# Sliding attention with the values stationary: two heads side by side, outputs transposed, probabilities normalised first

## The chip, the cores and the metric

One core of one Trainium2 chip runs the whole program in one launch. The metric is the device time of that launch in microseconds (us). PE is the matrix engine, PEld its weight loads, DVE the vector engine, ACT the scalar engine, POOL the general engine; SP only issues DMAs here.

## What is computed

The input is 256 tokens of width 1024 in fp32. Two layers of a first block (dilated and differential attention) are followed by two layers of a second block, and each of those runs two branches from one wide projection: a gated delta rule, and sliding attention with a sink, which is all that the change touches. Its 16 query heads of width 64 share 2 key/value heads, 8 to each; a query sees the 128 tokens up to and with itself.

```python
scores = einsum(qb, kw) * 64 ** -0.5            # 2 blocks of 128 queries
scores = where(mask, scores, -inf)              # 0 <= query - key < 128
m = maximum(max(scores), sink)                  # sink: one number per head
p = exp(scores - m)
probs = p / (sum(p) + exp(sink - m))
o = einsum(probs, vw)                           # 64 columns per head
y_b = o.reshape(256, 16 * 64) @ w_up_sw
...
mix = (sigmoid(gate_a) * y_a + sigmoid(gate_b) * y_b) @ w_o
x = x + rmsnorm(mix, post_mix_g)
ff = square(relu(rmsnorm(x) @ w_ff1)) @ w_ff2
x = x + rmsnorm(ff, post_mlp_g)
```

## The kernel before

All weights stream from HBM in pieces of 256 x 512. Each fp32 product of a projection is made of three matmuls in the faster fp32r format: a piece is split into `hi` (ACT, L284) and `lo` (DVE, L285), the activations are held as such a pair too (`lhi`, `llo`), and hi·hi, lo·hi and hi·lo are added up (L312 to L314, or L353 to L355 where the weights are the stationary operand). Three pieces of raw and four of split weights may be ahead of PE.

Everything that is not a projection is laid between the projection's matmuls by a planner in plain Python. `at(k, fn)` puts a step into a heap with a due time `k` units ahead, and `tick(0.5)` after every three-matmul step (after every six in the other form) moves the clock on and emits what has come due. So the due times alone set the order in which the instructions are written, and each engine runs its own instructions strictly in that order.

Sliding attention (`swa`, `windowed`) has two groups of 8 heads in each layer, and a head has four steps, with a new head every 2.1 units:

- `s_`: four fp32r matmuls give the scores (L495, L496); DVE masks them and takes their maxima (L500, two instructions with two register reads) and works out the bias of the exponent (`nm`, L1276).
- `e_`, 1.5 units later: ACT writes the exponentials into the tile `e` (L1284, 128 queries by 256 keys for the second block of queries, by 128 for the first) and their sums into `den`; POOL adds the sink's share to `den` (L1288).
- `t_`, at 2.8: PE turns `e` in three transposes (L507), ACT copies the result to SBUF as `ptS` (L509).
- `v_`, at 3.7: three fp32 matmuls (L513 to L515) hold 128 x 128 blocks of the turned probabilities stationary and move 64 columns of `vS` past them. The output `o` has queries on partitions.

After every fourth head DVE takes the reciprocals of 8 sums (L1303) and scales `o` into the tile `y`, named `tok` in the profile (L1305, twice). After every eighth head `to_lh` turns two blocks of `y`: four transposes (L371), a copy by ACT to `lhi` (L376) and the rest by DVE to `llo` (L378). The pair `lb` is then the input of the projection by `w_up_sw`.

Besides the attention the same stretch holds the delta rule's work: the convolution (L990, L993), small inversions of triangular matrices (L1138 to L1192) and the turned queries `qk` (L446, L461, L462). PSUM gives three buffers to the short-lived results of all these (tag `wk`, with scores, transposes and inversions), four to the projections and one to `o`.

Of the kernel before, what the change touches and what calls it, by code (L numbers as in the profile page):

```python
# [12 lines left out]
F32 = mybir.dt.float32  # L13
F32R = mybir.dt.float32r
I32 = mybir.dt.int32
AF = mybir.ActivationFunctionType
ALU = mybir.AluOpType
# [60 lines left out]
def body(ctx: ExitStack, tc: tile.TileContext, I, out, upto=None):  # L78
    nc = tc.nc
    V, S, G, T = nc.vector, nc.scalar, nc.gpsimd, nc.tensor  # L80
# [22 lines left out]
    def tb_(name):  # L103
        o, n = _WHERE[name]
        return tab[:, o - n0:o - n0 + n]
# [25 lines left out]
    def wk(shape, name="wk", tag="wk", bufs=3):  # L131
        return ps.tile(shape, F32, name=name, tag=tag, bufs=bufs)
# [52 lines left out]
    rope2 = [const.tile([128, 2, 16], F32, name=n) for n in ("cc2", "ss2")]  # L185
# [45 lines left out]
    def at(k, fn):  # L231
        heapq.heappush(due, (clk[0] + k, seq[0], fn))
        seq[0] += 1
# [7 lines left out]
    def tick(n=1.0):  # L241
        feed()
        pump(clk[0] + n)
# [6 lines left out]
    def tiny(n, name="tiny", bufs=4):  # L250
        return sm.tile([128, n], F32, name=name, tag=f"{name}{n}", bufs=bufs)
# [46 lines left out]
    def piece():  # L298
        if not splits:
            feed()  # L300
        return splits.popleft()

    def release():
        count["done"] += 1

    def acc2():
        return [ps.tile([128, 512], F32, name="acc", tag="acc", bufs=4) for _ in range(2)]
# [8 lines left out]
    def proj(lh, evac, sweep=False):  # L316

        acc = acc2()
        if not sweep:
            for c in range(8):  # L320
                if c % 2 == 0:
                    hi, lo, n = piece()
                for t in range(2):
                    mm3(acc[t], n, lh, c, t, hi, lo, c % 2, c == 0, c == 7)
                    if t and c % 2:
                        release()
                    if c == 7:
                        evac(acc[t], t)
                    tick(0.5)
        else:  # L330
            pieces = []
            for t in range(2):
                for c in range(8):
                    if t == 0 and c % 2 == 0:
                        pieces.append(piece())
                    hi, lo, n = pieces[c // 2]
                    mm3(acc[t], n, lh, c, t, hi, lo, c % 2, c == 0, c == 7)
                    if t and c % 2:
                        release()
                    if c == 7:  # L340
                        evac(acc[t], t)
                    tick(0.5)
# [24 lines left out]
    def to_lh(lh, src, c0, t, scale=None):  # L367

        p = wk([128, 4, 128], "tp")
        for a in range(4):  # L370
            T.transpose(p[:, a, :], src[:, a * 128:(a + 1) * 128], ident)  # L371
        sl = slice(t * 128, (t + 1) * 128)
        if scale is None or isinstance(scale, float):
            s = 1.0 if scale is None else scale
            h = lh[0][:, c0:c0 + 4, sl]
            S.activation(h, p, AF.Copy, scale=s)  # L376
            if scale is None:
                V.tensor_tensor(out=lh[1][:, c0:c0 + 4, sl], in0=p, in1=h.bitcast(F32), op=ALU.subtract)  # L378
            else:
                for a in range(4):  # L380
                    V.scalar_tensor_tensor(lh[1][:, c0 + a, sl], p[:, a, :], s, lh[0][:, c0 + a, sl].bitcast(F32),
                                           op0=ALU.mult, op1=ALU.subtract)
        else:
            for a in range(4):
                S.activation(lh[0][:, c0 + a, sl], p[:, a, :], AF.Copy, scale=scale[:, c0 + a:c0 + a + 1])  # L385
            for a in range(4):
                w = scale[:, c0 + a:c0 + a + 1]
                V.scalar_tensor_tensor(lh[1][:, c0 + a, sl], p[:, a, :], w, lh[0][:, c0 + a, sl].bitcast(F32),  # L388
                                       op0=ALU.mult, op1=ALU.subtract)
# [61 lines left out]
    def halves(i):  # L451
        return slice(64 * i, 64 * i + 64), slice(64 - 64 * i, 128 - 64 * i)

    def into_stack(dst, r, tabs):


        def then(p, cols, t):
            for i in range(2):
                a, b = halves(i)
                h = dst[a, i:8:2, cols]  # L460
                S.activation(h, p[a], AF.Copy)  # L461
                V.tensor_tensor(out=dst[b, i:8:2, cols], in0=p[a], in1=h.bitcast(F32), op=ALU.subtract)  # L462
        return turned(r, tabs, then, 4)
# [23 lines left out]
    SPL = ((0, 256), (256, 384))  # L487
# [16 lines left out]
    def probs_T(p):  # L504
        pt = wk([128, 384], "pt")
        for j in range(3):
            T.transpose(pt[:, j * 128:(j + 1) * 128], p[:, j * 128:(j + 1) * 128], ident)  # L507
        r = sm.tile([128, 384], F32, name="ptS", tag="ptS", bufs=2)
        S.activation(r, pt, AF.Copy)  # L509
        return r  # L510

    def pv_mm(o1, o0, pt, v, cols):
        T.matmul(o1, pt[:, 0:128], v[:, 0, cols], start=True, stop=False)  # L513
        T.matmul(o1, pt[:, 128:256], v[:, 1, cols], start=False, stop=True)
        T.matmul(o0, pt[:, 256:384], v[:, 0, cols], start=True, stop=True)  # L515
# [359 lines left out]
    def layer2(l, last):  # L875
        lh = nxt["lh"]
# [6 lines left out]
        vS = act.tile([128, 2, 128], F32, name="vS", tag="vS", bufs=1)  # L883
# [380 lines left out]

        lane = [0.0]

        def windowed(q, g, y):
            st = {}

            def s_(h):  # L1270
                if h % 4 == 0:
                    st["den", h // 4] = tiny(8, "den")
                s, mx = scores(q[:, h, :], kTs[0][:, g, :], kTs[1][:, g, :], tb_("bs"))
                nm = tiny(2, "nm")
                hs = 8 * g + h
                V.tensor_scalar(nm, mx, -0.125, nsink[:, hs:hs + 1], op0=ALU.mult, op1=ALU.min)  # L1276
                st["s", h] = s, nm

            def e_(h):
                den, i, hs = st["den", h // 4], h % 4, 8 * g + h  # L1280
                s, nm = st.pop(("s", h))
                e = e_tile()
                for j, (a, b) in enumerate(SPL):
                    S.activation(e[:, a:b], s[:, a:b], AF.Exp, bias=nm[:, j:j + 1], scale=0.125,  # L1284
                                 accum_out=den[:, 2 * i + j:2 * i + j + 1])
                es = tiny(2, "es")
                S.activation(es, nm, AF.Exp, bias=sinks[:, 16 * l + hs:16 * l + hs + 1])
                G.tensor_tensor(out=den[:, 2 * i:2 * i + 2], in0=den[:, 2 * i:2 * i + 2], in1=es, op=ALU.add)  # L1288
                st["p", h] = e

            def t_(h):
                st["pt", h] = probs_T(st.pop(("p", h)))

            def v_(h):
                hh, i = h // 4, h % 4
                if i == 0:
                    st["o"] = wk([128, 4, 2, 64], "o", "o", 1)
                o = st["o"]
                pv_mm(o[:, i, 0, :], o[:, i, 1, :], st.pop(("pt", h)), vS, slice(64 * g, 64 * g + 64))
                if i < 3:  # L1300
                    return
                rd = tiny(8, "rd")
                V.reciprocal(rd, st["den", hh])  # L1303
                for j in range(2):
                    V.tensor_tensor(out=y[:, 1 - j, 256 * hh:256 * hh + 256].rearrange("p (h d) -> p h d", d=64),  # L1305
                                    in0=o[:, :, j, :],
                                    in1=rd.rearrange("p (h t) -> p t h", t=2)[:, j, :, None].to_broadcast([128, 4, 64]),
                                    op=ALU.mult)
                if hh == 1:
                    for t in range(2):  # L1310
                        at(1.6 + t, lambda t=t: to_lh(sw["lb"], y[:, t, :], 4 * g, t))

            for h in range(8):
                k = max(4, lane[0] - clk[0])
                at(k, lambda h=h: s_(h))
                at(k + 1.5, lambda h=h: e_(h))
                at(k + 2.8, lambda h=h: t_(h))
                at(k + 3.7, lambda h=h: v_(h))
                lane[0] = clk[0] + k + 2.1

        m1, fins, end = [], [], 0.0
# [5 lines left out]
        sw = {}  # L1327

        def swa(g):
            q = qk_tile([8, 256], F32R)  # L1330
            if g == 0:
                sw["lb"] = new_lh()
            y, evac = into_stack(q, None, rope2)
            proj(lh, evac)
            windowed(q, g, y)

        for hh in range(2):
            qkn = dn_qk(hh)
# [43 lines left out]
        lh, r = nxt["lh"], nxt["r"]  # L1382
# [111 lines left out]
    p = wk([128, 512])  # L1494
# [50 lines left out]
```

## Time and profile before

| | us |
|---|---|
| median of 3 runs | 1742.82 |
| the runs | 1741.65 to 1745.22 |
| the profiled execution | 1741.27 |
| its span | 1739.5 |

The span is what the profiler saw between the first and the last instruction of that one execution, 1.8 us less than its time. Start times below count from the start of the span; a duration is one instruction's or that of several merged ones (x3). Ends of matmuls are modelled and overlap the next, so what a matmul costs on PE is read from the starts of neighbours. The mean granted TensorE clock is 0.99 of full speed. The second block's sliding attention is spread over 840 to 950 us in the first of its layers, and over 1357 to 1470 us in the second.

### The profile page before, as it was taken

The numbers are of one execution on the slowest core, as the hardware profiler recorded it, in microseconds if no ns is written. First come the engines' busy times: TensorE is split into PE (matmuls) and PEld (weight loads), VectorE is DVE, ScalarE is ACT, GpSimd is POOL, SyncE is SP. The second block draws the span as 40 slices with busy tenths as digits, with TensorE's granted clock in tenths as the row PEclk, the third lists the DMA queues.
The fourth block names the chain that finished last, engine by engine and source line by source line (L and its number), as shares of the span: only waits on it lengthen the run. The fifth ranks groups of instructions, "written<-read, shape, count | busy, mean of one in ns | idle before, by whom it ended". The sixth has DMA issues, their size and how long they took to land.

```text
span 1739.5 us, 26865 instructions
## 1 busy us (share of the span) xinstructions
PE 1705.6 (98%) x9865; PEld 1484.6 (85%) x9865; DVE 1169.9 (67%) x2189; ACT 996.4 (57%) x1786; POOL 268.1 (15%) x507
## 2 busy tenths in 40 slices
PE   8999999999999999999999999999999999999998
PEld 6788888888888888898889889998998888889997
DVE  5676776666777766788585676555788584775554
ACT  6666665466666654665665455445565666464443
POOL 2112321031123200320220000000320210010000
PEclk9999999999999999999999999999999999999999
DMA  6655465466655565554332655665554333646564
GB/s 206 196 173 167 152 189 173 159 195 181 177 164 155 172 192 174 168 166 134 96 104 86 197 167 182 194 193 170 160 170 140 87 102 93 198 158 195 184 184 140
DMA packets 158932, 282.27 MB, mean 162 GB/s; under 512 B 20560, under 2 KB 28496, under 8 KB 158800
## 3 DMA queue, kind: packets, MB, share of 16 engines
q1 hardware_dynamic: 157840, 277.83, 53.0%
q0 software_dynamic: 720, 2.62, 0.4%
q8 instruction: 78, 1.28, 0.3%
q14 instruction: 54, 0.44, 0.1%
q10 hardware_dynamic: 240, 0.09, 0.0%
HBM read 270.53 MB, written 1.59 MB: 156 GB/s over the span
## 4 chain that ended last, share of the span: by engine, by line
PE 51%; DVE 5%; issue 1%; ACT 1%; POOL 0%; DMA 0%; DVEq 0%; POOLq 0%; SPq 0%; ACTq 0%
PE acc L314 6%; PE acc L312 6%; PE acc L313 6%; PE acc L353 5%; PE acc L354 5%; PE acc L355 5%; PE facc L313 3%; PE facc L312 3%; PE facc L314 3%; DVE lo L285 2%; DVE hcv L993 1%; PE inv L1177 1%; PE inv L1167 1%; PE tp L371 1%; PE pt L507 1%
## 5 line engine op out<-in xcount | busy, mean ns | idle before, releaser
L285 DVE TENSOR_TENSOR lo<-raw,hi 128x1024 fp32r<-128x1024 f32 (+1 forms) x504 | 617.3, 1231 | 343.9 <-ACT hi L284 328.1
L284 ACT ACTIVATE hi<-raw 128x1024 fp32r<-128x1024 f32 (+1 forms) x504 | 527.3, 1052 | 357.5 <-PE acc L314 149.0
L312 PE MATMUL acc<-hi,lhi 128*128 128x512 f32 (+1 forms) x1344 | 550.4, 410 | 1.2 <-ACT lhi L385 1.2
L314 PE MATMUL acc<-hi,llo 128*128 128x512 f32 (+1 forms) x1344 | 526.2, 392 | 0.4 <-DVE llo L388 0.3
L313 PE MATMUL acc<-lo,lhi 128*128 128x512 f32 (+1 forms) x1344 | 524.2, 390 | 0.6 <-DVE lo L285 0.5
L314 PEld LDWEIGHTS acc<-hi,llo 128*128 128x128 f32 x1344 | 253.5, 189 | 57.4 <-DVE llo L388 3.4
L313 PEld LDWEIGHTS acc<-lo,lhi 128*128 128x128 f32 x1344 | 255.3, 190 | 41.3 <-DVE lo L285 2.0
L312 PEld LDWEIGHTS acc<-hi,lhi 128*128 128x128 f32 x1344 | 255.0, 190 | 39.7 <-ACT lhi L385 1.4
L353 PE MATMUL acc<-lhi,hi 128*128 128x256 f32 x832 | 239.1, 287 | 0.0
L355 PE MATMUL acc<-lhi,lo 128*128 128x256 f32 x832 | 235.4, 283 | 0.0
L354 PE MATMUL acc<-llo,hi 128*128 128x256 f32 x832 | 235.4, 283 | 0.0
L353 PEld LDWEIGHTS acc<-lhi,hi 128*128 128x128 f32 x832 | 159.5, 192 | 1.2 <-issue 0.4
L354 PEld LDWEIGHTS acc<-llo,hi 128*128 128x128 f32 x832 | 159.5, 192 | 0.7
L355 PEld LDWEIGHTS acc<-lhi,lo 128*128 128x128 f32 x832 | 159.4, 192 | 0.0
L312 PE MATMUL facc<-hi,fh 128*128 128x512 f32 x256 | 99.8, 390 | 0.0
L313 PE MATMUL facc<-lo,fh 128*128 128x512 f32 x256 | 99.8, 390 | 0.0
L314 PE MATMUL facc<-hi,fl 128*128 128x512 f32 x256 | 99.6, 389 | 0.0
L509 ACT ACTIVATE ptS<-pt 128x384 f32<-128x384 f32 x80 | 39.2, 490 | 82.0 <-PE pt L507 81.8
L546 POOL TENSOR_SCALAR pf<-pss 128x1 f32<-128x1 f32 x8 | 3.7, 458 | 467.6 <-ACT pj L860 467.6
L500 DVE CUSTOM_DVE_ANT_0 s<-sc,tab 128x256 f32<-128x256 f32 x192 | 60.4, 352 | 11.2 <-PE sc L496 10.6
L993 DVE SCALAR_TENSOR_TENSOR hcv<-acc,cw,hcv 128x255 f32<-128x255 f32 (+1 forms) x144 | 58.2, 475 | 1.5 <-ACT hcv L990 1.4
L314 PEld LDWEIGHTS facc<-hi,fl 128*128 128x128 f32 x256 | 48.1, 188 | 10.1
(306 smaller groups left out, 2206.9 us busy)
## 6 DMA issues: line engine op xcount, KB each, us to landing
raw<-in_w_in_dram SPq DMA_DIRECT2D x272, 512.0 KB, 3.8
raw<-in_w_ff_dram SPq DMA_DIRECT2D x128, 512.0 KB, 4.4
raw<-in_w_proj_a_dram SPq DMA_DIRECT2D x16, 512.0 KB, 3.9
raw<-in_w_proj_b_dram SPq DMA_DIRECT2D x16, 512.0 KB, 3.7
raw<-in_w_out_dram SPq DMA_DIRECT2D x16, 512.0 KB, 3.7
raw<-in_w_up_sw_dram SPq DMA_DIRECT2D x16, 512.0 KB, 3.7
raw<-in_w_up_dn_dram SPq DMA_DIRECT2D x16, 512.0 KB, 3.7
raw<-in_w_o_dram SPq DMA_DIRECT2D x16, 512.0 KB, 3.8
```

The costliest lines, as they stand in the source:

```text
L284: S.activation(hi[:, :, :o], raw[:, :, :o], AF.Copy)
L285: V.tensor_tensor(out=lo[:, :, :o], in0=raw[:, :, :o], in1=hi[:, :, :o].bitcast(F32), op=ALU.subtract)
L312: T.matmul(a, lh[0][:, c, sl], hi[:, cc, :n], start=first, stop=False)
L313: T.matmul(a, lh[0][:, c, sl], lo[:, cc, :n], start=False, stop=False)
L314: T.matmul(a, lh[1][:, c, sl], hi[:, cc, :n], start=False, stop=last)
L353: T.matmul(a, hi[:, c % 2, sl], lh[0][:, c, :], start=(c == 0 and m % 2 == 0), stop=False)
L354: T.matmul(a, hi[:, c % 2, sl], lh[1][:, c, :], start=False, stop=False)
L355: T.matmul(a, lo[:, c % 2, sl], lh[0][:, c, :], start=False, stop=(c == 7 and m % 2 == 1))
L371: T.transpose(p[:, a, :], src[:, a * 128:(a + 1) * 128], ident)
L500: V.tensor_tensor_reduce(s[:, a:b], sc[:, a:b], bias[:, a:b], 1.0, FMIN, ALU.add, ALU.max, accum_out=mx[:, j:j + 1])
L509: S.activation(r, pt, AF.Copy)
L993: V.scalar_tensor_tensor(ha[:, m, d:], a[:, m, :256 - d], tap(3 - d, m), ha[:, m, d:], op0=ALU.mult, op1=ALU.add)
```

## The change

The order of the product is turned round. The values of one key/value head, 64 columns of `vS`, are the stationary operand, and the turned probabilities move past them, so the output has the head's 64 dimensions on partitions and queries in the free dimension. That is the layout of `lhi` and `llo` already. Two heads share the array: the first uses columns 0 to 63 and partitions 0 to 63 of `o`, the second the other half. A pair of heads has four matmuls, two that move 256 columns (L1312) and two that move 128 (L1315). After every fourth head ACT writes two pieces of `lhi` (L1322) and DVE two of `llo` (L1323) straight from `o`. The tile `y`, the reciprocals and scalings by query (L1303, L1305) and the transposes of `to_lh` for this branch go.

Since queries are no longer on partitions there, the probabilities are divided by their sums before they are turned: the new step `n_`, 2.4 units after `s_`, takes the reciprocal of two sums (L1293) and scales `e` in place (L1295, once for 256 columns and once for 128), all on DVE. `t_` moves from 2.8 to 3.6 units, `v_` from 3.7 to 4.6, where it does its work at every second head only. Line numbers past L1330 are 12 higher than before. All in all PE has 8264 instructions in its order instead of 8336, DVE 1596 instead of 1512.

```diff
--- before.py
+++ after.py
@@ -1264,7 +1264,7 @@
 
         lane = [0.0]
 
-        def windowed(q, g, y):
+        def windowed(q, g):
             st = {}
 
             def s_(h):
@@ -1288,34 +1288,47 @@
                 G.tensor_tensor(out=den[:, 2 * i:2 * i + 2], in0=den[:, 2 * i:2 * i + 2], in1=es, op=ALU.add)
                 st["p", h] = e
 
+            def n_(h):
+                rd, i, e = tiny(2, "rd"), h % 4, st["p", h]
+                V.reciprocal(rd, st["den", h // 4][:, 2 * i:2 * i + 2])
+                for j, (a, b) in enumerate(SPL):
+                    V.tensor_scalar(e[:, a:b], e[:, a:b], rd[:, j:j + 1], None, op0=ALU.mult)
+
             def t_(h):
-                st["pt", h] = probs_T(st.pop(("p", h)))
+                st["pt", h] = probs_T(st.pop(("p", h))).rearrange("p (a c) -> p a c", a=3)
 
             def v_(h):
-                hh, i = h // 4, h % 4
-                if i == 0:
-                    st["o"] = wk([128, 4, 2, 64], "o", "o", 1)
-                o = st["o"]
-                pv_mm(o[:, i, 0, :], o[:, i, 1, :], st.pop(("pt", h)), vS, slice(64 * g, 64 * g + 64))
-                if i < 3:
+
+                if h % 2 == 0:
                     return
-                rd = tiny(8, "rd")
-                V.reciprocal(rd, st["den", hh])
-                for j in range(2):
-                    V.tensor_tensor(out=y[:, 1 - j, 256 * hh:256 * hh + 256].rearrange("p (h d) -> p h d", d=64),
-                                    in0=o[:, :, j, :],
-                                    in1=rd.rearrange("p (h t) -> p t h", t=2)[:, j, :, None].to_broadcast([128, 4, 64]),
-                                    op=ALU.mult)
-                if hh == 1:
-                    for t in range(2):
-                        at(1.6 + t, lambda t=t: to_lh(sw["lb"], y[:, t, :], 4 * g, t))
+                if h % 4 == 1:
+                    st["o"] = wk([128, 2, 256], "o", "o", 1)
+                o, pr = st["o"], h // 2 % 2
+                pts = [st.pop(("pt", h - 1)), st.pop(("pt", h))]
+                for blk in range(2):
+                    for i, pt in enumerate(pts):
+                        w = o[64 * i:64 * i + 64, pr, :]
+                        if blk == 0:
+                            T.matmul(w.rearrange("p (t c) -> p t c", t=2), vS[:, 0, 64 * g:64 * g + 64], pt[:, 0:3:2, :],
+                                     start=True, stop=False)
+                        else:
+                            T.matmul(w[:, 0:128], vS[:, 1, 64 * g:64 * g + 64], pt[:, 1, :], start=False, stop=True)
+                if pr == 0:
+                    return
+                c = 4 * g + 2 * (h // 4)
+                for t in range(2):
+                    hi, lo = [x[:, c:c + 2, 128 * t:128 * t + 128] for x in sw["lb"]]
+                    p = o[:, :, 128 - 128 * t:256 - 128 * t]
+                    S.activation(hi, p, AF.Copy)
+                    V.tensor_tensor(out=lo, in0=p, in1=hi.bitcast(F32), op=ALU.subtract)
 
             for h in range(8):
                 k = max(4, lane[0] - clk[0])
                 at(k, lambda h=h: s_(h))
                 at(k + 1.5, lambda h=h: e_(h))
-                at(k + 2.8, lambda h=h: t_(h))
-                at(k + 3.7, lambda h=h: v_(h))
+                at(k + 2.4, lambda h=h: n_(h))
+                at(k + 3.6, lambda h=h: t_(h))
+                at(k + 4.6, lambda h=h: v_(h))
                 lane[0] = clk[0] + k + 2.1
 
         m1, fins, end = [], [], 0.0
@@ -1330,9 +1343,8 @@
             q = qk_tile([8, 256], F32R)
             if g == 0:
                 sw["lb"] = new_lh()
-            y, evac = into_stack(q, None, rope2)
-            proj(lh, evac)
-            windowed(q, g, y)
+            proj(lh, into_stack(q, None, rope2)[1])
+            windowed(q, g)
 
         for hh in range(2):
             qkn = dn_qk(hh)
```

On DVE, in the middle of the first of the two layers, before the change: the scores of head 11 (L500, counted through the layer from 0), its `nm`, then a `to_lh` (L378) and the delta rule's L1158 ahead of a weight split.

```order
L993 SCALAR_TENSOR_TENSOR hcv<-acc,cw_80,hcv 128x254 x2
L993 SCALAR_TENSOR_TENSOR hcv<-acc,cw_80,hcv 128x253 x2
L500 ISA s,mx<-sc,tab 128x256
L500 ISA mx 128x1
L500 ISA s,mx<-sc,tab 128x128
L500 ISA mx 128x1
L1276 TENSOR_SCALAR nm<-mx,nsink 128x2
L378 TENSOR_TENSOR llo<-tp,lhi 128x4x128
L1158 TENSOR_TENSOR Xi<-Y,tab 128x512
L285 TENSOR_TENSOR lo<-raw,hi 128x1024
```

On DVE after the change, in the same place: L378 is gone, and behind the `nm` of head 11 and the delta rule's L1158 stand the three instructions of `n_` for head 10 (L1293, L1295).

```order
L993 SCALAR_TENSOR_TENSOR hcv<-acc,cw_80,hcv 128x254 x2
L993 SCALAR_TENSOR_TENSOR hcv<-acc,cw_80,hcv 128x253 x2
L500 ISA s,mx<-sc,tab 128x256
L500 ISA mx 128x1
L500 ISA s,mx<-sc,tab 128x128
L500 ISA mx 128x1
L1276 TENSOR_SCALAR nm<-mx,nsink 128x2
L1158 TENSOR_TENSOR Xi<-Y,tab 128x512
L1293 RECIPROCAL rd<-den 128x2
L1295 TENSOR_SCALAR e<-e,rd 128x256
L1295 TENSOR_SCALAR e<-e,rd 128x128
L285 TENSOR_TENSOR lo<-raw,hi 128x1024
```

So the scaling of head 10 stands on DVE behind the scores of head 11, and the split of weights has moved behind it.

On PE, the same place before the change: the scores of head 11, a `to_lh`, one step of a projection, and then the transposes of head 10 (L507).

```order
L495 MATMUL sc<-kTh,qk 128x256
L496 MATMUL sc<-kTl,qk 128x256
L495 MATMUL sc<-kTh,qk 128x256
L496 MATMUL sc<-kTl,qk 128x256
L371 MATMUL tp<-ident,tok 128x128 x4
L312 MATMUL acc<-hi,lhi 128x512
L313 MATMUL acc<-lo,lhi 128x512
L314 MATMUL acc<-hi,llo 128x512
L507 MATMUL pt<-ident,e 128x128 x3
L312 MATMUL acc<-hi,lhi 128x512
L313 MATMUL acc<-lo,lhi 128x512
L314 MATMUL acc<-hi,llo 128x512
```

On PE after the change: the transposes of head 10 stand three projection steps behind the scores of head 11 (the last of these steps is shown), and one step and the scores of head 12 follow.

```order
L312 MATMUL acc<-hi,lhi 128x512
L313 MATMUL acc<-lo,lhi 128x512
L314 MATMUL acc<-hi,llo 128x512
L507 MATMUL pt<-ident,e 128x128 x3
L312 MATMUL acc<-hi,lhi 128x512
L313 MATMUL acc<-lo,lhi 128x512
L314 MATMUL acc<-hi,llo 128x512
L495 MATMUL sc<-kTh,qk 128x256
L496 MATMUL sc<-kTl,qk 128x256
L495 MATMUL sc<-kTh,qk 128x256
L496 MATMUL sc<-kTl,qk 128x256
```

The transposes now read an `e` that DVE has scaled, so they depend on the rows of `n_` shown above and no longer on ACT alone; a step of the projection and the scores of head 12 are queued behind them on PE.

On PE, the product with the values for one head before the change, between two projection steps:

```order
L314 MATMUL acc<-hi,llo 128x512
L513 MATMUL o<-vS,ptS 128x64
L514 MATMUL o<-vS,ptS 128x64
L515 MATMUL o<-vS,ptS 128x64
L312 MATMUL acc<-hi,lhi 128x512
```

On PE, the product for a pair of heads after the change, between a projection step and the inversions:

```order
L314 MATMUL acc<-hi,llo 128x512
L1312 MATMUL o<-ptS,vS 64x256 x2
L1315 MATMUL o<-ptS,vS 64x128 x2
L1167 MATMUL inv<-Xi,LA 128x128 x4
L312 MATMUL acc<-hi,lhi 128x512
```

One block of three matmuls per head has become one block of four per two heads, with another shape of the array than its neighbours.

## Rows read from the trace of the kernel before

**Rows 1.** The page, busy time of each engine in the whole span

```profile
PE 1705.6 (98%) x9865; PEld 1484.6 (85%) x9865; DVE 1169.9 (67%) x2189; ACT 996.4 (57%) x1786; POOL 268.1 (15%) x507
```

**Rows 2.** Windows of both layers: length, busy time (instructions) by engine, PEclk, DMA

```profile
880.00:900.00 20.00, 19.56 (x154) 18.14 (x153) 17.55 (x51) 13.10 (x35) 3.54 (x7) 1.00 0.35 91
900.00:920.00 20.00, 19.14 (x133) 17.11 (x133) 16.88 (x45) 13.09 (x35) 1.49 (x3) 1.00 0.36 104
1397.00:1417.00 20.00, 19.57 (x154) 18.13 (x154) 17.53 (x51) 13.11 (x35) 3.45 (x7) 1.00 0.35 92
```

**Rows 3.** Timeline of DVE: start, duration, line, out<-in, [idle before <-releaser]

```profile
879.73 1.23 DVE L285 TENSOR_TENSOR lo<-raw,hi 128x1024 fp32r<-128x1024 f32 x1 [0.88 <-ACT hi L284]
...
889.31 0.68 DVE L462 TENSOR_TENSOR qk<-tp,qk 64x512 fp32r<-64x512 f32 x1 [0.30 <-ACT qk L461]
...
896.30 0.23 DVE L1276 TENSOR_SCALAR nm<-mx,nsink 128x2 f32<-128x2 f32 x1
...
906.36 0.42 DVE L500 CUSTOM_DVE_ANT_0 s<-sc,tab 128x256 f32<-128x256 f32 x1
...
907.17 0.68 DVE L378 TENSOR_TENSOR llo<-tp,lhi 128x512 fp32r<-128x512 f32 x1
907.77 0.68 DVE L1158 TENSOR_TENSOR Xi<-Y,tab 128x512 f32<-128x512 f32 x1
```

**Rows 4.** Timeline of PE in the same stretch

```profile
892.26 0.70 PE L507 MATMUL pt<-ident,e 128*128 128x128 f32 x3
...
901.02 0.28 PE L495 MATMUL sc<-kTh,qk 128*128 128x256 f32 x1
...
903.65 0.52 PE L507 MATMUL pt<-ident,e 128*128 128x128 f32 x3 [0.86 <-DVE llo L378]
```

**Rows 5.** Timeline of PE: a product with the values, a block of transposes

```profile
874.39 0.33 PE L513 MATMUL o<-vS,ptS 128*128 128x64 f32 x2
...
874.98 0.47 PE L312 MATMUL acc<-hi,lhi 128*128 128x512 f32 x1
875.29 0.39 PE L313 MATMUL acc<-lo,lhi 128*128 128x512 f32 x1
...
898.46 0.66 PE L371 MATMUL tp<-ident,tok 128*128 128x128 f32 x4
898.88 0.47 PE L312 MATMUL acc<-hi,lhi 128*128 128x512 f32 x1
```

**Rows 6.** Timeline: fp32 matmuls on 8 columns of the array, and the next load

```profile
746.31 0.60 PE L942 MATMUL tp<-tab,gd 128*8 128x256 f32 x2
...
746.75 0.38 PE L943 MATMUL tp<-tab,gd 128*8 128x128 f32 x2
...
747.06 0.19 PEld L353 LDWEIGHTS acc<-lhi,hi 128*128 128x128 f32 x1 [0.22 <-issue]
```

**Rows 7.** Timeline of DVE in the first block: a reciprocal and scalings of `e`

```profile
593.71 0.18 DVE L714 RECIPROCAL rdb<-denb 128x4 f32<-128x4 f32 x1 [0.53 <-ACT e L708]
593.93 0.23 DVE L715 TENSOR_SCALAR rdb<-rdb,lams 128x2 f32<-128x2 f32 x1
594.19 0.35 DVE L719 TENSOR_SCALAR e<-e,rdb 128x256 f32<-128x256 f32 x1
594.58 0.49 DVE L720 SCALAR_TENSOR_TENSOR pc<-e,rdb 128x256 f32<-128x256 f32 x1
594.99 0.28 DVE L719 TENSOR_SCALAR e<-e,rdb 128x128 f32<-128x128 f32 x1
```

**Rows 8.** Timeline of DVE: the scaling by query of four heads

```profile
897.57 0.20 DVE L1303 RECIPROCAL rd<-den 128x8 f32<-128x8 f32 x1
897.87 0.76 DVE L1305 TENSOR_TENSOR tok<-o,rd 128x256 f32<-128x256 f32 x2
```

**Rows 9.** Windows around an idle stretch of PE in the delta rule, columns as in rows 2

```profile
802.00:804.00 2.00, 1.05 (x9) 1.05 (x10) 1.97 (x4) 1.58 (x2) 0.00 (x0) 1.00 0.58 224
804.00:808.00 4.00, 3.95 (x16) 2.84 (x15) 3.97 (x5) 1.02 (x3) 0.00 (x0) 0.57 0.51 144
```

## The prediction

> **What bounds the kernel now.** I read the page's busy times first: PE is busy for 98% of the span and DVE for 67% [rows 1]. By that alone, work taken off PE is gain and work put on DVE is free. The second view, windows of 20 us over the sliding attention, says that the average hides two cases. In 880 to 920 us DVE is busy for 17.55 and 16.88 of 20 us, in both layers alike (17.53 in the second), while PE is at 19.56 and 19.14 [rows 2]. This is where the delta rule's inversions fall between the heads.
>
> The third view is DVE's own timeline there. Its last wait for a weight split ends at 879.73 [rows 3]; from then to about 909 us it idles only in three short waits for ACT, of which the 0.30 us at 889.31 is one. So it falls behind: PE writes the scores of head 11 at 901.02 [rows 4], and DVE comes to them at 906.36 [rows 3], 5.3 us later. Today PE feels little of that. The transposes of a head, L507, need only ACT's exponentials, which need DVE's `nm` of that same head, and that was issued long before. PE's one stall is 0.86 us at 903.65, where the transposes of head 10 wait for DVE to free a PSUM buffer (L378) [rows 4]. That is the place to ask what a further dependence of PE on DVE costs.
>
> **PE, removed and added.** One fp32 matmul shows as two passes (x2). A product with the values takes from 874.39 to 874.98, so 0.59, and the fp32r matmul behind it needs 0.31 to its neighbour (874.98 to 875.29) where these take 0.23 in a row, so 0.08 more: 0.67 per head [rows 5]. A block of four transposes in `to_lh` takes 0.42 (898.46 to 898.88) and again 0.08: 0.50 [rows 5]. A layer has 16 products and 4 such blocks, 16 x 0.67 + 4 x 0.50 = 12.7 us.
>
> No row of before shows two heads on two halves of the array. The nearest are fp32 matmuls on 8 columns of it: 256 moved columns take 0.44 (746.31 to 746.75), 128 take 0.22 to 0.31 with the return to the whole array (to 747.06, 0.22 of it idle in the load of weights) [rows 6]. A pair of heads has two of each, 2 x (0.44 + 0.22) = 1.32 if the halves run one after the other; 0.66 if they run at once; and 0.88 if only neighbours in the order overlap. With 0.17 for the two changes of shape that is 1.49, 0.83 or 1.05, and for 8 pairs 11.9, 6.6 or 8.4. I take 1.05, between the two. So PE saves 4.3 us a layer, with bounds of 0.8 and 6.1.
>
> The row on the return to the whole array shows weights that are loaded only after 0.22 us of idle [rows 6]. The Trainium skill, "TensorEngine Tiling (Array Packing)", Key Properties, says that a change of the tiling mode drains the engine, which speaks against the change: 16 such drains a layer. At 0.22 each instead of the 0.08 taken above they would cost 16 x 0.14 = 2.2 us a layer more.
>
> **DVE, added and removed.** The first block does the same scaling of `e` in the same shapes. From the reciprocal to the next instruction is 0.22, from the scaling of 256 columns to the next 0.39, and the one of 128 takes 0.28 and the gap of 0.03: 0.92 us per head [rows 7], 29 us in 32 heads. From below it could be 0.81, the bare durations. Each head's transposes on PE now depend on it. Of four heads' end, a reciprocal and two scalings go, 0.96 (0.20 + 0.76) [rows 8]; L378, 0.60 to the next start [rows 3], goes twice in eight heads. L1323 comes twice per four heads, from PSUM, 256 elements: taken as L1305, 0.76 a pair.
>
> **Where it lands.** In the new order `n_` of a head stands behind the scores and `nm` of the next. For head 10 that is behind `nm` of head 11 and a further L1158, and PE has the transposes of head 10 three projection steps behind the scores of head 11. In before DVE ends that L1158 at 907.77 + 0.68 = 908.45 [rows 3]. The new order has the same instructions ahead of `n_` of head 10, and these besides:
>
> - `n_` of heads 6 to 10: 5 x 0.92 = 4.60.
> - Ahead of the split at 879.73, `n_` of head 5 and a pair of L1323 (0.92 + 0.76), of which the idle 0.88 there [rows 3] swallows a part: + 0.80.
> - A second pair of L1323: + 0.76. Gone are a reciprocal with two scalings, - 0.96, and two L378, - 1.20.
> - The `n_` of head 7 stands among the four L462 and fills the wait of 0.30 at 889.31 [rows 3]: - 0.30. The other two waits remain, since there ACT and DVE take turns on one tile.
>
> 908.45 + 4.60 + 0.80 + 0.76 - 0.96 - 1.20 - 0.30 = 912.15. PE, by the pace of before, would be ready for these transposes after two projection steps past 903.65, at 903.65 + 0.31 + 5 x 0.23 = 905.1 [rows 4, 5]. So PE is 7.05 us late there. Most of that falls earlier: the transposes of head 8, which PE reaches at 892.26 [rows 4], now wait for DVE's `n_` behind the `nm` that ends at 896.53 [rows 3], 4 us or more. What PE had saved until then is lost, since it only waits longer. What it saves after that point counts: seven products against four pairs, 7 x 0.67 - 4 x 1.05 = 0.5, and two blocks of `to_lh`, 1.0. Net 7.05 - 1.5 = 5.55 us a layer, if DVE never idles in between; but it now also waits for scores that a stalled PE writes later. Two or three such waits of the size of the present ones (0.3 to 0.9) [rows 3] would make it 7.2. I take 6.3 a layer, 12.6 for two.
>
> Behind it DVE has room, and nothing in the projections needs the attention's result soon, so the loss is neither made good nor grows.
>
> **The clock.** After PE stood idle for almost half of 802 to 804, the granted clock was 0.57 over the next 4 us, between the levels of 1.2 and 2.4 GHz, so 4 x 0.43 = 1.7 us of full speed were lost [rows 9]. The idle 0.86 at 903.65 cost nothing of the kind: the clock is 1.00 in that window [rows 2]. The new stalls are of 2 us and more, long enough to expect a fall, but one that comes while DVE is the bound anyway is hidden. I count one of two layers: 1.7.
>
> Sum: 1741.27 + 12.6 + 1.7 = 1755.6 for an execution like the profiled one. The median of the runs is 1.55 above that, so I forecast 1757 us, 14.3 slower.
>
> **Rivals.**
>
> - *PE's savings show (chance 0.14).* If `n_` costs much less than 0.92, or DVE catches up before PE comes to the transposes, then PE's sum alone counts: 2 x 4.3 = 8.6 faster, 1734 us; with halves that fully overlap 12.2, so 1731. For it speaks PE's 98% [rows 1]; against it the lag of 5.3 us that DVE has already without `n_`.
> - *Little changes (0.09).* Half of the lag is absorbed because the new waits let DVE's other work move up, and PE's savings cover the rest, or the halves run one after the other (0.8 a layer) and DVE keeps up: 1739 to 1746.
> - *The halves don't run at once and the stalls are dearer (0.17).* With 1.49 a pair the gain after the stall turns from 0.5 to 7 x 0.67 - 4 x 1.49 = -1.3, so 1.8 a layer more, with a clock fall in each layer 1.7 more, and with the upper 7.2 per layer: 1742.8 + 2 x (7.2 + 1.8 + 1.7) = 1764.
> - *The halves overlap even in the order given.* The Trainium skill, "TensorE: Matmul & The Clock Gate", Part 3, has column tiles run together, three of them 2.38 times as fast as in turn. No row here shows two matmuls on two halves; by it a pair would cost 0.83, and the forecast would be 2 x 4 x 0.22 = 1.8 lower. It is part of the forecast's range.
>
> The forecast itself has 0.60, with its own range of 1749 to 1762: below by a DVE price of 0.81 (5 x 0.11 a layer) and no fall of the clock, above by the 7.2 and two falls. About 0.2% (3.5 us) is what can be told from no change. Faster by more than that: 0.17, the first rival and a part of the second. Within: 0.08. Slower: 0.75. The range of 8 in 10 goes from 1737 to 1764.
>
> **What would show it.** Right: PE's L507 for heads 7, 8 and 10 waits for DVE's L1295 by 2 to 5 us each; PE's busy time in 880 to 920 falls by several us while DVE comes near 19 of 20; L1295 takes 0.35 and 0.28. L1312 of the second head starting before the first's ends shows overlap, with 0.83 to 1.05 from a pair's first start to the next projection matmul; 1.49 shows that there is none. Wrong, if L507 waits for no DVE row, if L1295 takes half the time, or if DVE's scores of head 11 come no later against PE than 5.3 us.

## The result, and the profile after

| | before | after |
|---|---|---|
| median, us | 1742.24 (4 runs) | 1770.57 (4 runs) |
| lowest to highest | 1740.8 to 1745.2 | 1768.8 to 1773.6 |
| ratio, 95% interval | | 1.0162 (1.0142 to 1.0182) |
| span of the profiled run | 1739.5 | 1767.0 |

The change makes the kernel 28.3 us slower. The direction and the place were forecast; of the size only half was (14.3 us), and the measured time lies above the range, which ended at 1764.

One slip of the prediction first: it counts the heads one too high. Its heads 5 to 11 are heads 4 to 10 counted from 0, in all its places alike, so no term depends on it; the section on the change counts as it does. Below, heads are counted from 0.

The page's busy times show nothing of the loss; PE works as long as before [rows 1]:

```profile
PE 1705.4 (97%) x9769; PEld 1473.8 (83%) x9769; DVE 1181.9 (67%) x2269; ACT 996.2 (56%) x1794; POOL 270.7 (15%) x507
```

Windows of the kernel after, two for each layer, in the columns of rows 2:

```profile
880.00:900.00 20.00, 13.08 (x96) 11.90 (x95) 16.35 (x50) 10.62 (x26) 4.53 (x10) 0.90 0.28 81
900.00:920.00 20.00, 15.27 (x78) 13.37 (x79) 14.56 (x43) 8.93 (x27) 2.19 (x3) 0.76 0.31 84
1410.00:1430.00 20.00, 12.44 (x103) 11.44 (x101) 15.72 (x46) 11.59 (x28) 5.13 (x11) 1.00 0.30 81
1430.00:1450.00 20.00, 14.37 (x73) 12.28 (x74) 14.69 (x46) 8.65 (x26) 2.19 (x3) 0.80 0.34 92
```

PE has gone from 19.56 and 19.14 to 13.08 and 15.27 of 20 us [rows 2], the second layer likewise. DVE was expected near 19 and fell too, to 16.35 and 14.56: the two now wait for each other. And the granted clock is 0.90, 0.76 and 0.80 where it was 1.00.

What PE waited for in the first layer (836 to 970 us), after: total us, times, longest. The last row is the second layer's (1355 to 1490).

```profile
PE pt L507 <- DVE e L1295: 12.1, 6, 4.7
PE inv L1177 <- ACT Z L1169: 0.6, 1, 0.6
...
PE tp L1048 <- DVE Y L1180: 0.3, 1, 0.3
...
PE pt L507 <- DVE e L1295: 13.6, 6, 4.7
```

Before, the wait of L507 for DVE in the same stretch was the one of 0.86 us [rows 4]. Four of the six waits of the first layer in the timeline of PE after, and the scores of head 10:

```profile
884.36 0.52 PE L507 MATMUL pt<-ident,e 128*128 128x128 f32 x3 [2.44 <-DVE e L1295]
...
892.07 0.52 PE L507 MATMUL pt<-ident,e 128*128 128x128 f32 x3 [0.50 <-DVE e L1295]
...
899.91 0.87 PE L507 MATMUL pt<-ident,e 128*128 128x128 f32 x3 [3.98 <-DVE e L1295]
...
907.54 0.28 PE L495 MATMUL sc<-kTh,qk 128*128 128x256 f32 x1
...
914.97 0.88 PE L507 MATMUL pt<-ident,e 128*128 128x128 f32 x3 [4.73 <-DVE e L1295]
```

The waits are those of heads 5, 6, 7 and 9. And DVE's side of the lockstep, its timeline after:

```profile
883.65 0.17 DVE L1293 RECIPROCAL rd<-den 128x2 f32<-128x2 f32 x1 [0.70 <-POOL den L1288]
883.86 0.55 DVE L1295 TENSOR_SCALAR e<-e,rd 128x256 f32<-128x256 f32 x2
884.32 0.15 DVE L1138 TENSOR_TENSOR Y<-Y 64x2 f32<-64x2 f32 x1
...
902.90 0.42 DVE L500 CUSTOM_DVE_ANT_0 s<-sc,tab 128x256 f32<-128x256 f32 x1 [1.80 <-PE sc L496]
...
912.86 0.42 DVE L500 CUSTOM_DVE_ANT_0 s<-sc,tab 128x256 f32<-128x256 f32 x1
...
913.67 0.69 DVE L1158 TENSOR_TENSOR Xi<-Y,tab 128x512 f32<-128x512 f32 x1
914.27 0.16 DVE L1293 RECIPROCAL rd<-den 128x2 f32<-128x2 f32 x1
914.47 0.55 DVE L1295 TENSOR_SCALAR e<-e,rd 128x256 f32<-128x256 f32 x2
```

`n_` takes 884.32 - 883.65 = 0.67 us, less than the 0.92 taken from rows 7. PE's wait for head 9 ends with DVE's row at 914.47, which stands behind L1158 as the order says. At 902.90 DVE has caught up and waits 1.80 us for scores that PE, held up by head 7, writes late. One sign that the prediction named for being wrong did come: DVE reaches the scores of head 10 at 912.86, 5.3 us behind PE (907.54), no later than before. The sign was badly chosen, since a PE that is held up itself writes its scores later.

Product with the values for a pair, timeline of PE after:

```profile
903.29 0.28 PE L355 MATMUL acc<-lhi,lo 128*128 128x256 f32 x1
903.50 0.65 PE L1312 MATMUL o<-ptS,vS 128*64 128x256 f32 x4
903.98 0.39 PE L1315 MATMUL o<-ptS,vS 128*64 128x128 f32 x4
904.30 0.39 PE L353 MATMUL acc<-lhi,hi 128*128 128x256 f32 x1
904.52 0.28 PE L354 MATMUL acc<-llo,hi 128*128 128x256 f32 x1
```

904.30 - 903.50 = 0.80 us for both heads: the halves run at once. Ahead of it 0.21 and behind it 0.22 pass where 0.12 is usual, so the changes of shape cost 0.19, and a pair 0.99 in all (1.05 was forecast, 1.34 was before). The two heads side by side cost little here; the loss lies elsewhere.

The clock in the trace of after, in windows of 2 us behind the waits for heads 7 and 9:

```profile
900.00:902.00 2.00, 2.00 (x10) 2.00 (x11) 1.09 (x1) 1.12 (x4) 0.00 (x0) 0.50 0.15 29
914.00:916.00 2.00, 1.03 (x4) 1.03 (x5) 1.96 (x5) 0.06 (x1) 0.00 (x0) 0.50 0.00 0
916.00:918.00 2.00, 2.00 (x9) 1.74 (x8) 0.15 (x1) 1.49 (x6) 0.20 (x1) 0.50 0.33 44
918.00:920.00 2.00, 2.00 (x10) 1.96 (x10) 1.49 (x8) 0.28 (x1) 0.00 (x0) 0.57 0.58 218
```

0.50 is 1.2 GHz. In the first layer the clock falls behind each of the three long waits, and PE's matmuls there take twice as long. In the second it stays up in 1410 to 1430 and falls later. The windows of 20 us above give an estimate of what that lost at full speed: 20 x (0.10 + 0.24 + 0.20) = 10.8 us.

### The profile page after: what moved, and what is told of

Read it like the earlier page. It is cut to its first block, busy times and chain, and to the rows that moved or that the text cites. A ratio compares the mean times of both kernels' runs of the same rounds, so it can differ in the third digit from the quotient of the medians.

```text
span 1767.0 us, 26766 instructions
## 1 busy us (share of the span) xinstructions
PE 1705.4 (97%) x9769; PEld 1473.8 (83%) x9769; DVE 1181.9 (67%) x2269; ACT 996.2 (56%) x1794; POOL 270.7 (15%) x507
## 4 chain that ended last, share of the span: by engine, by line
PE 43%; DVE 9%; ACT 3%; issue 2%; POOL 1%; DMA 1%; SPq 0%; DVEq 0%; POOLq 0%; ACTq 0%
PE acc L314 5%; PE acc L312 5%; PE acc L313 5%; PE acc L353 4%; PE acc L355 4%; PE acc L354 4%; PE facc L312 3%; PE facc L313 3%; PE facc L314 3%; DVE lo L285 3%; DVE hcv L993 2%; PE inv L1177 1%; PE inv L1167 1%; ACT hi L284 1%; DMA rw<-gr 1%
## 5 line engine op out<-in xcount | busy, mean ns | idle before, releaser
L500 DVE CUSTOM_DVE_ANT_0 s<-sc,tab 128x256 f32<-128x256 f32 x192 | 60.4, 352 | 13.5 <-PE sc L496 12.8
L993 DVE SCALAR_TENSOR_TENSOR hcv<-acc,cw,hcv 128x255 f32<-128x255 f32 (+1 forms) x144 | 58.2, 474 | 3.6 <-ACT hcv L990 3.6
```

The lines of the kernel that those rows point to most:

```text
L500: V.tensor_tensor_reduce(s[:, a:b], sc[:, a:b], bias[:, a:b], 1.0, FMIN, ALU.add, ALU.max, accum_out=mx[:, j:j + 1])
L993: V.scalar_tensor_tensor(ha[:, m, d:], a[:, m, :256 - d], tap(3 - d, m), ha[:, m, d:], op0=ALU.mult, op1=ALU.add)
```

## The experiments

The theory (W): PE's transposes wait for `n_` on a DVE that is late, and the clock falls behind the waits. Its rivals: the array's shapes cost the time (M); DVE's added load costs it whether anyone waits for `n_` or not (L); and, for the clock alone, that its falls are hidden behind DVE. Times are medians; a ratio is to the kernel before on the same chip, with its 95% interval.

| kernel | us | ratio |
|---|---|---|
| without `n_` | 1738.73 | 0.9984 (0.9970 to 0.9998) |
| `n_` aside | 1751.89 | 1.0051 (1.0035 to 1.0068) |
| transposes later | 1752.69 | 1.0054 (1.0034 to 1.0074) |
| before, with `n_` | 1763.61 | 1.0124 (1.0099 to 1.0148) |
| idle work, one head late | 1778.90 | 1.0200 (1.0179 to 1.0220) |
| idle work, at the waits | 1761.64 | 1.0103 (1.0086 to 1.0119) |
| `n_` on ACT | 1756.71 | 1.0071 (1.0044 to 1.0097) |
| `n_` on ACT, all later | 1751.18 | 1.0040 (1.0028 to 1.0052) |
| `n_` on POOL, all later | 1745.37 | 1.0015 (1.0004 to 1.0025) |
| `n_` on POOL, less late | 1744.30 | 1.0006 (0.9997 to 1.0015) |
| `n_` on POOL, all later, idle work | 1749.58 | 1.0034 (1.0021 to 1.0046) |
| heads in turn | 1767.86 (one run) | |

**Without n_.** The division is left out.

```diff
             def n_(h):
-                rd, i, e = tiny(2, "rd"), h % 4, st["p", h]
-                ...
+                return
```

> The changed kernel without its step n_ (this leaves the division by the sums out). Theory W (waits): the loss is PE's transposes waiting for n_ on a late DVE, with the falls of the clock behind these waits. Then only PE's saving is left: a pair of heads costs about 0.98 in the trace of after against 1.34, so 8 x 0.36 + 4 x 0.50 = 4.9 us a layer: 1742.2 - 9.8 = 1732 us, and no wait of L507 for DVE over 1 us. Rival M (modes): the array's halves and the changes of shape cost the time, some way the trace doesn't show: then it stays near 1770. Rival L (load): DVE's added work as such costs the time: also 1732 here, told apart by the next kernel.

Measured 1738.73. The loss goes with `n_`, so M is out. But PE's saving of 9.8 us brings only 2.8 (0.16% of 1741). What PE waited for in its first layer shows why:

```profile
PE sc L495 <- DVE qk L462: 2.0, 2, 1.7
PE inv L1167 <- DVE Xi L1158: 0.9, 1, 0.9
PE inv L1167 <- ACT ptS L509: 0.7, 1, 0.7
```

A PE with less to do comes to the next thing too early: 1.7 us for the turned queries of the second group, which ACT and DVE make by turns, and at the inversions. So in 880 to 911 PE waits for DVE already without `n_`.

**n_ aside.** The same DVE work, into a tile that nobody reads; the result lacks the division.

```diff
+                en = sm.tile([128, 256], F32, name="en", tag="en", bufs=1)
-                    V.tensor_scalar(e[:, a:b], e[:, a:b], rd[:, j:j + 1], None, op0=ALU.mult)
+                    V.tensor_scalar(en[:, 0:b - a], e[:, a:b], rd[:, j:j + 1], None, op0=ALU.mult)
```

> The changed kernel with n_ in its place and with all its work, but written to a tile of its own that nobody reads (the division is left out of the result). DVE's load stays, PE's dependence on it goes. Theory W: 1732 to 1738 us, since PE waits for DVE only through PSUM buffers. Rival L: the load alone keeps the time at 1762 or more. Rival M: 1770.

Measured 1751.89, between the two theories: 1.0051 - 0.9984 = 0.67%, 11.7 us, is DVE's load without the dependence. It reaches PE through what DVE has always owed it, the turned queries and PSUM buffers:

```profile
PE sc L495 <- DVE qk L462: 2.9, 2, 2.6
PE pt L507 <- DVE mx L500: 1.7, 1, 1.7
```

The clock falls behind these waits too, in both layers alike (1410 to 1430 is also at 0.83):

```profile
880.00:900.00 20.00, 15.29 (x108) 14.08 (x107) 15.22 (x43) 12.03 (x29) 4.87 (x11) 0.83 0.27 80
```

By an estimate from these windows that is up to 2 x 20 x 0.17 = 6.8 of the 11.7 us; no run parts it from the load itself. The rest up to the changed kernel, 1.0162 - 1.0051, 19.3 us, is the dependence. By the intervals each of the two differences is good to some 4 us.

**Transposes later.** Nothing is left out.

```diff
...
-                at(k + 3.6, lambda h=h: t_(h))
-                at(k + 4.6, lambda h=h: v_(h))
+                at(k + 6.0, lambda h=h: t_(h))
+                at(k + 7.0, lambda h=h: v_(h))
-        return sm.tile([128, 384], F32, name="e", tag="e", bufs=3)
+        return sm.tile([128, 384], F32, name="e", tag="e", bufs=4)
...
```

> The changed kernel, complete, with the transposes and the product with the values 2.4 planner units (3.4 us of PE work) later: t_ at 6.0, v_ at 7.0, and four buffers of e for three. Theory W: waits of 2.4, 4.0 and 4.7 us become 0, about 0.6 and 1.3 to 2, so the clock falls at most once a layer: 1738 to 1748 us. Rival L: DVE's load is the same, so 1762 or more. Rival M: 1770.

Measured 1752.69, the same as with `n_` aside: slack in the order takes the whole dependence away and none of the load. The forecast of 1738 to 1748 took DVE's load for free and missed; rival L's 1762 or more took it for the whole loss and missed too. No L507 waits for L1295 any more; PE waits where DVE's load shows:

```profile
PE sc L495 <- DVE qk L462: 3.5, 2, 3.2
PE inv L1167 <- ACT ptS L509: 2.7, 1, 2.7
```

**Before, with n_.**

```diff
+                at(k + 2.4, lambda h=h: n_(h))
-                at(k + 2.8, lambda h=h: t_(h))
-                at(k + 3.7, lambda h=h: v_(h))
+                at(k + 3.6, lambda h=h: t_(h))
+                at(k + 4.6, lambda h=h: v_(h))
...
-                    V.tensor_tensor(out=y[...], in0=o[:, :, j, :], in1=rd..., op=ALU.mult)
+                    V.tensor_copy(y[...], o[:, :, j, :])
```

> The kernel before, with nothing changed but that the probabilities are normalised ahead: n_ at 2.4, t_ at 3.6, v_ at 4.6 as in the changed kernel, L1305 as plain copies. Theory W: the same waits with none of PE's savings behind them: 1772 to 1782 us. Rival M: the normalisation is harmless by itself, 1742 to 1750. Rival L: as W.

Measured 1763.61: the normalisation ahead costs 21.6 us by itself, which settles M again. W's 1772 to 1782 was too high: it added PE's missing saving to the changed kernel's time, but this kernel is some 7 us faster than that one. Its waits for `n_` are shorter, as PE's waits in the first layer show, and its clock falls less, as the window of 900 to 920 shows (880 to 900 is at 1.00):

```profile
PE pt L507 <- DVE e L1295: 7.6, 5, 2.6
```

```profile
900.00:920.00 20.00, 14.98 (x95) 13.44 (x95) 17.86 (x49) 10.02 (x26) 2.19 (x3) 0.91 0.33 86
```

So with `n_` in both, the turned product makes the kernel slower, although it takes work off PE. That fits a stretch which DVE bounds, where work taken off PE comes back as idle time and costs clock besides. The idle time is argued here; the next runs test the clock.

**Idle work on PE.** The changed kernel, with matmuls into the buffer that the transposes overwrite.

```diff
-    def probs_T(p):
+    def probs_T(p, idle=0):
         pt = wk([128, 384], "pt")
+        for _ in range(idle):
+            T.matmul(pt[:, 0:128], ident, ident, start=True, stop=True)
...
-                st["pt", h] = probs_T(st.pop(("p", h)))...
+                st["pt", h] = probs_T(st.pop(("p", h)), {6: 10, 8: 16, 10: 20}.get(8 * g + h, 0))...
```

> The changed kernel, complete, with idle work on PE: ahead of the transposes of the layer's heads 6, 8 and 10, where PE waited 2.44, 3.98 and 4.73 us, stand 10, 16 and 20 fp32 matmuls of the identity with itself, 2.2, 3.5 and 4.4 us at 0.22 each, into the buffer that the transposes overwrite. Theory C (clock): behind these waits matmuls run at half pace for about 2.8, 2.6 and 4.5 us, 5 us a layer lost; kept busy, PE keeps its clock: 1770.6 - 2 x 4 to 5 = 1761 to 1763 us, although it has 20 us more work. Rival: the falls are hidden behind DVE, which is the bound there, so 1770 or, with work that fits badly, up to 1775.

Measured 1778.90: a miss of the set-up. By the prediction's count the work stood one head too late, ahead of transposes that hardly wait; the three long waits stayed (2.43, 2.47, 2.92 us), and the work came on top. With `{5: 10, 7: 16, 9: 20}` instead:

> The idle work on PE again, now ahead of the transposes that really wait longest, those of heads 5, 7 and 9 counted from 0 (2.44, 3.98, 4.73 us in the changed kernel); the earlier run had it one head too late. 10, 16 and 20 fp32 matmuls of the identity with itself, 1.2, 1.8 and 2.3 us by the earlier run's trace (32 passes in 3.6 us). Theory C: the clock stays up behind these waits, the matmuls there run at 0.12 and 0.23 from start to start instead of 0.21 and 0.43, and DVE's next scores come earlier: 1770.6 - 2 x 3 to 5 = 1761 to 1765 us. Rival: the falls are hidden behind DVE: 1769 to 1773 with the same 5 us of added work in the waits.

Measured 1761.64: with 46 matmuls more in each layer the kernel is 8.9 us faster by the medians, and 10.3 us by the ratios (1.0162 - 1.0103), which compare each kernel with before on its own chip (this difference too is good to some 4 us). Windows of the first layer, PE's timeline at head 7, and DVE's next scores:

```profile
880.00:900.00 20.00, 17.46 (x149) 16.46 (x147) 16.57 (x50) 10.38 (x26) 4.37 (x9) 1.00 0.29 83
900.00:920.00 20.00, 19.83 (x144) 17.27 (x143) 15.04 (x44) 11.17 (x30) 2.19 (x3) 1.00 0.31 83
```

```profile
895.54 3.73 PE L507 MATMUL pt<-ident 128*128 128x128 f32 x32
899.62 0.55 PE L509 MATMUL pt<-ident,e 128*128 128x128 f32 x3 [0.35 <-DVE e L1297]
...
901.39 0.42 DVE L500 CUSTOM_DVE_ANT_0 s<-sc,tab 128x256 f32<-128x256 f32 x1 [0.50 <-PE sc L496]
```

The transposes start at 899.62, where they started at 899.91: the idle work lies wholly in the wait. What differs is the clock, 1.00 instead of 0.90 and 0.76, and with it DVE's wait for the scores behind these transposes, 0.50 instead of 1.80. So the falls are not hidden; they are worth some 9 to 10 of the 28.3 us.

**n_ off DVE.** On ACT, with a reciprocal on POOL:

```diff
...
+                G.tensor_tensor(out=st["rd", h], in0=den[:, 2 * i:2 * i + 2], in1=none_c, op=ALU.pow)
...
-                V.reciprocal(rd, st["den", h // 4][:, 2 * i:2 * i + 2])
...
-                    V.tensor_scalar(e[:, a:b], e[:, a:b], rd[:, j:j + 1], None, op0=ALU.mult)
+                    S.activation(e[:, a:b], e[:, a:b], AF.Copy, scale=st["rd", h][:, j:j + 1])
```

> The changed kernel, complete, with n_ off DVE: POOL takes the reciprocal of the sums (a power of -1) and ACT scales e in place. Theory W+L (DVE's load costs some 6 us a layer, the wait for DVE some 9): both go, what is left is the time without n_, 1738.7, plus waits for ACT and POOL: 1739 to 1746 us. Rival: ACT takes DVE's place, since the exponentials, the copies of ptS and the weight splits are in its queue: 1750 or more.

> As the kernel before in this list, with n_ at 3.2, t_ at 6.0, v_ at 7.0 and four buffers of e: also the wait of PE for ACT's scaling goes. Theory W+L: 1737 to 1742 us, the best complete version. Rival (ACT's load): as the one before, no better.

Measured 1756.71, and with `n_` at 3.2, `t_` at 6.0 and `v_` at 7.0 1751.18: both miss the forecast. In the first ACT takes DVE's place, as the rival has it, and PE waits for ACT's scaling. The second is 5.5 us better, though the intervals overlap; whether ACT's load is what is left there isn't shown, since PE waits for DVE again, for the queries and for a PSUM buffer (last row):

```profile
PE pt L508 <- ACT e L1297: 7.7, 3, 3.1
```

```profile
PE inv L1168 <- DVE mx L501: 2.7, 2, 2.5
```

Then all of `n_` on POOL, at the later times:

```diff
-                    S.activation(e[:, a:b], e[:, a:b], AF.Copy, scale=st["rd", h][:, j:j + 1])
+                    G.tensor_scalar(e[:, a:b], e[:, a:b], st["rd", h][:, j:j + 1], None, op0=ALU.mult)
```

> The changed kernel, complete, with n_ on POOL altogether: reciprocal (a power of -1) and both scalings of e there, n_ at 3.2, t_ at 6.0, v_ at 7.0, four buffers of e. DVE and ACT carry nothing of it. If what is left of the loss in the version with ACT (1751 us) is ACT's and DVE's load, this comes to the time without n_: 1738 to 1743 us. Rival: POOL is slow at it (L1102 takes 0.96 for 256 columns, so 1.4 us a head and the power of 0.6 besides) and holds DVE up while both work on SBUF: 1748 or more, with DVE's rows next to POOL's drawn out.

Measured 1745.37, between expectation and rival, 0.15% above before. POOL has the time, though its rows are drawn out at some places, as here 2.56 against 1.51 us:

```profile
899.31 2.56 POOL L1297 TENSOR_SCALAR e<-e,rd 128x256 f32<-128x256 f32 x2
...
902.92 1.51 POOL L1297 TENSOR_SCALAR e<-e,rd 128x256 f32<-128x256 f32 x2
```

DVE's rows are not drawn out, against the rival: making the queries (L462, here L463) takes 0.69 us at the median, as in the changed kernel.

The same with `t_` at 5.0 and `v_` at 6.0:

> The version with n_ on POOL (1745.4 us), t_ at 5.0 and v_ at 6.0 instead of 6.0 and 7.0. POOL's three instructions take about 2.4 us, so e is ready at about 3.2 + 1.8 = 5.0 units; PE waited 2.06 us for ACT's ptS at one place, where late transposes meet the inversions. If that bunching is what is left, 1741 to 1744 us; if the transposes now wait for POOL instead, 1746 to 1752.

Measured 1744.30, ratio 1.0006 (0.9997 to 1.0015): the same as before, at the edge of what was expected. It is the best version that leaves nothing out, and it is no faster than the kernel before. And the late version with idle work ahead of the scores of head 8 (the same edit as above, in `scores`):

> The version with n_ on POOL (1745.4 us), with 16 fp32 matmuls of the identity with itself ahead of the scores of head 8, where PE waits 2.06 us for DVE's qk and the granted clock in 880 to 900 is 0.91: 1.8 us of idle work into the buffer that the scores overwrite. Theory C: the clock stays at 1.00 there, 20 x 0.09 = 1.8 us less a layer: 1741 to 1743 us. Rival: the wait is DVE's and ends when it ends: 1745 to 1747.

Measured 1749.58, worse by 4.2. The idle work reads only the identity, yet waited 1.36 us, so most likely for the PSUM buffer that it shares with the scores; it came behind the wait and was only more work. The clock in 880 to 900 was 1.00 in the profiled execution, but what that is worth this run can't tell:

```profile
887.17 3.81 PE L495 MATMUL sc<-ident 128*128 128x128 f32 x32 [1.36 <-DVE qk L463]
```

**Heads in turn.** The order of the four matmuls of a pair.

```diff
-                for blk in range(2):
-                    for i, pt in enumerate(pts):
+                for i, pt in enumerate(pts):
+                    for blk in range(2):
```

> The changed kernel with the four matmuls of a pair in another order: both of the first head, then both of the second. If matmuls on the two halves overlap when they are neighbours in the order, a pair takes 0.44 + 0.22 + 0.44 + 0.22 less one overlap of up to 0.22, so 1.10 us from its first start to the next matmul, where it takes 0.80 now; if the halves don't overlap at all and the 0.80 has another reason, 0.80 again.

The pair takes 903.14 - 902.33 = 0.81 us again, but not for the reason given: the halves overlap, and not only between neighbours in the order. The trace has the passes of both L1312 ahead of those of L1315, though one L1315 is written between them:

```profile
902.33 0.66 PE L1312 MATMUL o<-ptS,vS 128*64 128x256 f32 x4
902.81 0.39 PE L1315 MATMUL o<-ptS,vS 128*64 128x128 f32 x4
903.14 0.39 PE L353 MATMUL acc<-lhi,hi 128*128 128x256 f32 x1
```

## Why the prediction was right in kind and wrong in size

Two terms of the sum were too small: what PE's lateness costs, "I take 6.3 a layer", and the clock, 1.7. PE was to come 7.05 us late in a layer; it waited 12.1 and 13.6 us for `n_`, and the falls of the clock are worth some 9 to 10 us. Step by step:

- *DVE, late in 880 to 911, becomes what PE waits for* was right, by place (L507 on L1295) and cause; `n_` aside and the later transposes show the cause. Of the heads, 7 and 9 were right (3.98 and 4.73 us); head 6 waits 0.50 where 2 to 5 were expected, and the 2.44 of head 5 was not forecast.
- *The order on DVE decides when head 9's e is ready* was right; the chain was forecast to end at 912.15 and ended at 914.47 + 0.55 = 915.02, 2.9 late. `n_` was cheaper than taken (5 x 0.25 = 1.3 less) and the start 0.3 later, so the waits that DVE met were larger: 3.6 us instead of the 1.65 that separate 5.55 from 7.2, with 1.80 for scores, 0.70 for POOL's `den`, and 0.83 at L1323 and 0.30 at L993 for ACT. The step allowed for them as small; it overlooked that a stalled PE with a halved clock writes the next scores later still (with the clock kept up the 1.80 is 0.50).
- *The clock: "I count one of two layers: 1.7"* is the step that failed most. The idle work at the waits shows 9 to 10 us. Waits of 2.05 to 4.74 us come three to the first layer and four to the second, and most of the falls behind them were not hidden: what PE does behind a wait (the scores) is what DVE waits for next.
- *"What it saves after that point counts": 1.5 a layer* failed. With `n_` in both, the turned product makes the kernel some 7 us slower and not 3 faster (before, with `n_`). Even without `n_`, PE's whole saving of 4.9 a layer shows as 1.4, near the 1.5 by luck: PE's waits in the first layer add up to 4.2 us there against 1.9 before, the most of it for the queries and at the inversions. The prediction asked what is late next for DVE and did not ask it for PE's saving.
- *The price of a pair* was right (0.99 for 1.05). The two changes of shape cost 0.19 a pair. By the rule of the Trainium skill, "TensorEngine Tiling (Array Packing)", Key Properties, each drains the engine; the trace agrees that there is a price, and it is small. The other rule weighed, that of the Trainium skill, "TensorE: Matmul & The Clock Gate", Part 3, has column tiles run together, and the trace agrees: 0.80 us for what would be 1.32 in turn.
- The sum in these parts: 28.3 = -2.8 (the change without `n_`) + 11.7 (DVE's load) + 19.3 (the dependence), with 0.1 of rounding. The clock's 9 to 10 us lie in the last two together. The forecast had -3.0 for PE's work, 15.6 for the lateness and 1.7 for the clock; the top of the range allowed one fall in each layer, 3.4 us. Its narrower range of 1749 to 1762 doesn't follow from the terms that it names, which give about 1754 to 1760.

What stays open: how much of DVE's load and how much of the dependence is clock, what makes the clock fall behind one wait and not another (below), and why POOL's rows are drawn out at some places.

## What to carry to other kernels

A new dependence of the busiest engine on another has to be priced at the place where that other engine is latest, and the lateness feeds back: the waiting engine writes its own results later, and its clock may fall besides. Where a second engine bounds a stretch, work taken off the first saves little (2.8 of 9.8 us here). What helped is slack between the two (later consumers, 1752.69 us), and slack together with moving the new work to an engine that was mostly idle, even where each pair of instructions takes nearly three times as long (1.51 us on POOL for 0.55 on DVE; 1744.30 us).

## What was not expected of the hardware

- Idle work ahead of a wait made the kernel some 9 to 10 us faster; what it changed is the granted clock (1.00 against 0.90 and 0.76 in the same windows).
- The length of a wait alone doesn't tell whether the clock falls. In the changed kernel it fell behind 2.44 us in the first layer (0.90 in 880 to 900) and not behind 2.44 us at the same place in the second (1.00 in 1410 to 1430). Behind 3.21 us it didn't fall either, in the kernel with later transposes, where PE's wait for the queries ends at 895.88; with `n_` aside the wait at this place is 2.63 us, and it did (0.83 in 880 to 900, above). In the kernel with later transposes:

```profile
892.00:896.00 4.00, 0.79 (x6) 0.46 (x6) 3.00 (x7) 1.33 (x3) 0.00 (x0) 1.00 0.26 98
896.00:898.00 2.00, 2.00 (x17) 1.87 (x17) 1.45 (x3) 1.98 (x5) 0.00 (x0) 1.00 0.00 0
```

- Matmuls on two column halves start out of the program's order: with the heads in turn, the second head's L1312 ran with the first's, ahead of the L1315 that is written before it.
